# Tree attention on one core: twelve partitions of three stores go to SyncE's queue, and turn 17 has one transposition instead of two

## The chip, the cores and the metric

The kernel runs on one core of a Trainium2 chip. Its time is the device time of one execution in microseconds (us), and less is better. Three runs of the kernel before gave 132.96 us as their median (132.62 to 134.33).

## What is computed

Inputs are Q, K and V of shape (8, 12, 512, 64) in 4-byte floats: 96 independent heads of 512 rows. Row i stands for a node of a binary tree, and it may look at itself and at its ancestors only:

```python
    for i in range(seq):
        mask[i, i] = 1
        parent = i
        while parent > 0:
            parent = (parent - 1) // 2
            mask[i, parent] = 1

    scores = np.einsum('bhqd,bhkd->bhqk', Q, K) * scale
    scores = scores + (1 - mask) * (-1e9)

    weights = np.exp(scores - np.max(scores, axis=-1, keepdims=True))
    weights = weights / (np.sum(weights, axis=-1, keepdims=True) + 1e-10)

    return np.einsum('bhqk,bhkd->bhqd', weights, V).astype(np.float32)
```

## The kernel before

A partition p of the 128 holds the four rows 4p to 4p + 3 of a head, so that a head's row of output is 1 KB in a partition. The 96 heads go in 48 pairs (index i in the code), and four pairs form a group of eight heads (g = i // 4).

**Loads.** POOL (GpSimd) issues nearly all transfers, in the order that the string POOL (L612) writes out. Each load of K, Q or V for eight heads (`load_coarse` at L262, `load` at L251) turns the 4-byte values into 2-byte ones on the way. POOL also copies in SBUF: parts of V are spread into the layout that the products need (`spread`, L306, tile vt), and K and Q of a group are laid side by side (`lay_beside`, L324, tiles Kbeside and Qbeside).

**Transpositions.** For a group, four steps T of eight transposes each on TensorE (PE) fill the PSUM tile kqp: two steps for the keys (L375) and two for the queries (L397). VectorE (DVE) copies the result to the SBUF tile kq: after each key step by a copy of 1024 elements a partition (L444), and after the second query step by one of 2048 (L436). There is no copy after the first query step. There is one buffer for kqp.

**Scores, values, norm.** A step S computes the scores of a pair in PSUM (L494, L499, L519, L525) and ScalarE (ACT) takes their exponentials (L510, L541). A step V multiplies them with V into the PSUM tile ob (L552), and DVE divides by the sums (L585, L590) into the SBUF tile `of`, one for each of the groups 0 to 10, and into a small tile `ol` for each of the last four pairs. There is one buffer for ob.

**The order.** The string EARLY (L726) writes out the first steps. From then on a loop over turns i (L767) does "S T V": scores of pair i, the next transposition in line, values of pair i - 1. TURNS (L727) replaces the order of single turns. With one T a turn, the transposition made in turn i is number i + 4, so that a group's last one falls in the turn just before the scores that read it. In the kernel before, turn 17 has two of them, "S T V T", and from turn 18 on the transposition of turn i is number i + 5; turn 43 has none left.

**Stores.** `store` (L597) writes the output of a group of eight heads, 1 MB, in one DMA. POOL issues the eleven of them, s0 to s10 in the string POOL, s0 behind the load v88 and the last ones when nothing else is left. The last four pairs are stored by `store_pair` (L604): two from POOL, one and a half from SyncE (SP), half a one from ACT. SP otherwise issues two small loads at the start.

Of the kernel before, what the change touches and what calls it, by code (L numbers as in the profile page):

```python
# [11 lines left out]
CODE_ROWS = 40  # L12
CODE_BITS = 16
NOUT = 10
COARSE = range(1, 12)
COARSE_K = range(1, 12)
BESIDE = {"K": range(3, 12), "Q": range(3, 12)}
# [104 lines left out]
def kernel(  # L122
# [7 lines left out]
    nc = tc.nc  # L130
    B, H, S, D = Q.shape
    P = nc.NUM_PARTITIONS
# [5 lines left out]
    KB, VB = 8, 16  # L138
# [13 lines left out]
    Or = out.rearrange("b h (p t) d -> p (b h) (t d)", t=4)  # L152
# [14 lines left out]
    small = ctx.enter_context(tc.tile_pool(name="small", bufs=4))  # L167
    opool = ctx.enter_context(tc.tile_pool(name="opool", bufs=NOUT))
    olast = ctx.enter_context(tc.tile_pool(name="olast", bufs=GP))
# [61 lines left out]
    def head(i, a):  # L231

        g, x = divmod(i, GP)
        return KB * g + GP * a + x if g in COARSE else 2 * i + a

# [13 lines left out]
    qTs, kTs, kqps, obs, ets, ofs = {}, {}, {}, {}, {}, {}  # L249
# [12 lines left out]
    def load_coarse(kept, name, src, h0, n):  # L262

        assert n == KB
        issued.update((name, h) for h in range(h0, h0 + n))
        to = kept[h0 // KB] = loads.tile([P, 2, 16, D], bf16, name=name)
        return nc.gpsimd.dma_start(
            out=to[:, :, :, :].rearrange("p g s d -> p g (s d)"),
            in_=src[32 * h0:32 * (h0 + n), :].rearrange("(g r) c -> r g c", g=2),
        )  # L270
# [6 lines left out]
    def load_q(h0, n):  # L277
        if h0 // KB in COARSE:
            return load_coarse(qsts, "qst", Qc, h0, n)
        return load(qsts, loads, "qst", KB, Qr, h0, n)  # L280
# [29 lines left out]
    def lay_beside(copy, name, g):  # L310
# [4 lines left out]
        src = kept[:, :, :, :].bitcast(mybir.dt.uint32)  # L315
        if g not in COARSE:
            src = src.rearrange("p (x a) t w -> p x t a w", a=2)
        elif name == "Q" or g in COARSE_K:
            src = src.rearrange("p a s w -> p s a w")
        else:  # L320
            src = src.rearrange("p (a x) t w -> p (x t) a w", a=2)
        if g in COARSE:
            dst = dst.rearrange("p x t a w -> p (x t) a w")
# [53 lines left out]
    def transpose_coarse(i):  # L377

        g, x = divmod(i, GP)
        kqps[i] = kqps[i - 1] if x == 3 else psT.tile([P, 2, 32, 32], bf16, name="kqp")  # L380
        if x < 2 and g in COARSE_K:
            assert all(("kst", h) in issued for h in range(KB * g, KB * g + KB))
            return transpose_rows(i, x)
        if x < 2:
            for half in range(2):
                transpose_keys(GP * g + 2 * x + half, kqps[i], half)
            return
        assert all(("qst", h) in issued for h in range(KB * g, KB * g + KB))
        for half in range(2):
            for y, t in enumerate(ORDER):  # L390
                four = 2 * x - 4 + half
                for rows, src in turned(
                    "Q", g, t, lambda b: b[:, four, t, :, :], lambda a: qsts[g][:, a, 4 * four + t, :]
                ):
                    u = 16 * half + y
                    dst = kqps[i][rows, x - 2, u:u + 13:4, :]
                    nc.tensor.transpose(out=dst, in_=src, identity=eye[:, 0:128])  # L397

    def transpose(i, halves=(0, 1)):
        g = i // GP  # L400
        if g in COARSE:
            return transpose_coarse(i)
# [18 lines left out]
    def evac(i):  # L421
# [5 lines left out]
        if g in COARSE_K:  # L427
            dst = kqgs[g][:, 1, 2 * (x % 2):2 * (x % 2) + 2, :, :]
        elif g in COARSE:
            dst = kqgs[g][:, 2 * (x % 2):2 * (x % 2) + 2, x // 2, :, :]  # L430
# [164 lines left out]
            )  # L595

    def store(eng, g):  # L597
        return eng.dma_start(  # L598
            out=Or[:, KB * g:KB * g + KB, :],
            in_=ofs[g][:, :, :, :].rearrange("p h t d -> p h (t d)"),  # L600
        )


    def store_pair(eng, i, a=0, n=2):  # L604
# [14 lines left out]
    def pool_program():  # L619

        ops = []
        for word in POOL.split():
            kind, *n = word[0], *(int(x) for x in word[1:].split(".") if x)
            if kind in "kqv":
                h0, size = n if len(n) == 2 else (n[0], KB)
                ops.append(({"k": load_k, "q": load_q, "v": load_v}[kind], h0, size))
            elif kind in "KQ":
                ops.append((lay_early if kind == "K" else lay_q, n[0]))
            elif kind == "c":
                o, part, h0, h1 = n  # L630
                ops.append((spread, nc.gpsimd.tensor_copy, o, part, h0, h1))
            elif kind == "t":
                o, h0 = n
                ops += [
                    (spread, nc.gpsimd.tensor_copy, o, part, h0, h0 + KB)
                    for part in (6, 7, 8, 9) + ((), (4, 5))[min(o, 1)]
                ]
            elif kind == "s":
                ops.append((store, nc.gpsimd, n[0]))
            elif kind == "p":  # L640
                ops.append((store_pair, nc.gpsimd, n[0]))
            elif kind == "e":
                ops.append((eye_order,))
            else:
                ops.append((code_order, n[0]))
        return ops
# [77 lines left out]
        kept[0] = loads.tile([P, KB, 4, D], bf16, name=name)  # L724
        nc.vector.tensor_copy(out=kept[0][:, 0:2, :, :], in_=first[src][:, :, :, :])
    EARLY = "X K S Q D0 S A0 X6 T X D1 S X T V S T V T V T T A4 S D3 T V S T V"  # L726
    TURNS = {11: 'S T L4 V', 17: 'S T V T'}  # L727
    done, scored, valued = 1, 0, 0
    pool(-1)
    transpose(0)  # L730
# [36 lines left out]
    for i in range(scored, NP + 1):  # L767
        turn = "S T V" if i not in TURNS else TURNS[i]
        for token in turn.split():
# [39 lines left out]
```

## Time and profile before

| What | Value |
|---|---|
| Median of three runs | 132.96 us (132.62 to 134.33) |
| The profiled execution, its time | 132.84 us |
| The profiled execution, its span from first to last instruction | 130.8 us |
| Mean granted TensorE clock | 0.986 |
| PE busy | 115.4 us, 88% of the span |
| ACT busy | 99.0 us, 76% |
| POOL busy | 96.3 us, 74% |
| DVE busy | 95.9 us, 73% |
| DMA packets of POOL's queue | 30.67 MB moved, 23232 packets |
| Share of the chain that ended last | PE 59%, DVE 25%, POOL 6% |

The profile shows one execution. PE is the matmul unit, PEld its weight loads; SPq, POOLq and ACTq are the queues from which an engine issues. A row of a timeline has the start, the length, the engine, the line of the program, what is written and read, and a count; a bracket at its end names the idle time of the engine ahead of it and what ended that. In a table of stretches, a row has the stretch, its length, the busy time of PE, PEld, DVE, ACT and POOL with their counts of instructions, the granted clock of PE, the mean busy share of the 16 DMA engines (transfers overlap in an engine, so that it can be over 1) and the GB/s that they moved.

### The profile page before, as it was taken

What the parts mean: (1) busy time and instruction counts of PE and PEld (TensorE: products, weight loads), DVE (VectorE), ACT (ScalarE), POOL (GpSimd) and SP (SyncE); (2) the same over time, 40 slices, a digit from 0 to 9 for tenths busy, and PEclk for the clock granted to TensorE, in tenths of its full rate; (3) what the DMA queues carried; (4) which work ended last, traced back from release to release, by engine and by line L of the source; (5) the groups of instructions that cost most, each with busy time, mean ns of one, the idle gap of its engine ahead of it and who ended that gap; (6) DMA issues with size and microseconds to landing.
All of it is one profiled execution on the core that took longest, in us unless ns stands there. A gap on an engine that the chain in (4) does not pass through costs nothing.

```text
span 130.8 us, 4949 instructions
## 1 busy us (share of the span) xinstructions
PE 115.4 (88%) x2132; PEld 82.6 (63%) x2133; DVE 95.9 (73%) x179; ACT 99.0 (76%) x160; POOL 96.3 (74%) x149
## 2 busy tenths in 40 slices
PE   4989996999998998995999997989989999989930
PEld 1444565776866676774776875767767777856620
DVE  4236778758958959774989798798998898775460
ACT  4339553787988988886778886887897897899920
POOL 6979978239899999999999999999996930202300
PEclk9999999999999999999999999999999999999995
DMA  4999999999999999999999999999999999999992
GB/s 124 195 185 205 209 185 211 201 211 205 210 197 217 201 206 202 209 205 207 212 199 211 202 209 207 205 210 232 336 220 357 406 401 401 401 402 401 384 352 94
DMA packets 24533, 32.13 MB, mean 246 GB/s; under 512 B 944, under 2 KB 15920, under 8 KB 24512
## 3 DMA queue, kind: packets, MB, share of 16 engines
q0 software_dynamic: 23232, 30.67, 110.9%
q1 hardware_dynamic: 720, 0.70, 1.7%
q10 hardware_dynamic: 560, 0.46, 1.0%
q8 instruction: 16, 0.26, 0.7%
q14 instruction: 5, 0.04, 0.1%
HBM read 37.86 MB, written 12.58 MB: 385 GB/s over the span
## 4 chain that ended last, share of the span: by engine, by line
PE 59%; DVE 25%; POOL 6%; issue 3%; ACT 3%; ACTq 0%; POOLq 0%
PE ob L552 16%; DVE kq L436 7%; PE s L494 7%; DVE of L590 7%; PE kqp L375 7%; PE s L499 6%; PE kqp L397 6%; PE s L519 5%; DVE vt L306 5%; PE s L525 5%; PE s L718 3%; POOL vt L306 3%; PE ob L718 2%; PE kqp L350 2%; DVE rec L585 2%
## 5 line engine op out<-in xcount | busy, mean ns | idle before, releaser
L510 ACT ACTIVATE e<-s 128x1024 bf16<-128x1024 f32 x48 | 49.1, 1023 | 21.3 <-PE s L499 20.9
L306 POOL COPY vt<-vst 32x256 uint32<-32x256 uint32 (+2 forms) x70 | 34.9, 499 | 8.9 <-DMA vst<-in_V_dram 5.7
L541 ACT ACTIVATE e<-s 128x384 bf16<-128x384 f32 (+1 forms) x92 | 41.4, 505 | 0.0
L552 PE MATMUL ob<-vt,e 128*128 128x65 bf16 (+1 forms) x940 | 36.9, 197 | 2.4 <-DVE of L590 2.1
L552 PEld LDWEIGHTS <-e 128*128 128x128 bf16 (+1 forms) x960 | 31.2, 102 | 7.9 <-DVE of L590 3.7
L590 DVE TENSOR_TENSOR of<-ob,rec 128x512 f32<-128x512 f32 x44 | 30.4, 691 | 1.5
L306 DVE COPY vt<-vst 32x512 uint32<-32x512 uint32 (+1 forms) x33 | 20.6, 625 | 1.0
L499 PE MATMUL s<-kq 64*128 64x512 bf16 x96 | 18.4, 379 | 2.1 <-DVE kq L436 2.1
L525 PEld LDWEIGHTS <-kq 64*128 64x128 bf16 x384 | 16.3, 110 | 6.3
L598 POOL DMA_DIRECT2D out_dram<-of x11 | 9.8, 897 | 13.5 <-DVE of L590 13.5
L585 DVE RECIPROCAL rec<-ob 128x8 f32<-128x8 f32 x47 | 9.6, 204 | 12.8 <-PE ob L552 12.5
L444 DVE COPY kq<-kqp 128x1024 bf16<-128x1024 bf16 x22 | 15.1, 687 | 4.9 <-PE kqp L375 4.4
L525 PE MATMUL s<-kq 64*128 64x160 bf16 (+1 forms) x384 | 17.9, 210 | 0.0
L494 PE MATMUL s<-qcoarse,codes 40*128 40x512 bf16 x88 | 17.2, 387 | 0.0
L519 PE MATMUL s<-qcoarse,codes 40*128 40x480 bf16 x88 | 16.3, 364 | 0.3
L436 DVE COPY kq<-kqp 128x2048 bf16<-128x2048 bf16 x11 | 13.5, 1224 | 2.2 <-PE kqp L397 1.8
L375 PE MATMUL kqp<-mixed,Kbeside 128*128 128x128 bf16 x144 | 11.1, 220 | 2.8 <-POOL Kbeside L324 1.7
L519 PEld LDWEIGHTS <-codes 40*128 40x128 bf16 x96 | 7.6, 95 | 8.4 <-issue 2.0
L306 ACT COPY vt<-vst 32x512 uint32<-32x512 uint32 (+1 forms) x17 | 10.7, 627 | 1.7 <-DMA vst<-in_V_dram 1.3
L397 PE MATMUL kqp<-ptile,Qbeside 128*128 128x128 bf16 x144 | 11.2, 220 | 0.2 <-DVE kq L444 0.2
L375 PEld LDWEIGHTS <-Kbeside 128*128 128x128 bf16 x144 | 8.3, 98 | 4.2 <-POOL Kbeside L324 2.0
L257 POOL DMA_DIRECT2D vst<-in_V_dram x12 | 10.9, 910 | 0.0
(45 smaller groups left out, 102.2 us busy)
## 6 DMA issues: line engine op xcount, KB each, us to landing
out_dram<-of POOLq DMA_DIRECT2D x11, 1024.0 KB, 15.6
vst<-in_V_dram POOLq DMA_DIRECT2D x12, 512.0 KB, 14.0
kst<-in_K_dram POOLq DMA_DIRECT2D x11, 512.0 KB, 11.9
qst<-in_Q_dram POOLq DMA_DIRECT2D x11, 512.0 KB, 12.3
out_dram<-ol POOLq DMA_DIRECT2D x2, 256.0 KB, 5.3
qst<-in_Q_dram POOLq DMA_DIRECT2D x3, 128.0 KB, 7.1
ol<-in_K_dram SPq DMA_DIRECT2D x1, 256.0 KB, 2.9
ol<-in_Q_dram ACTq DMA_DIRECT2D x1, 256.0 KB, 3.2
```

Source lines behind the costliest of these rows:

```text
L306: return copy(out=dst, in_=src)
L375: nc.tensor.transpose(out=dst, in_=src, identity=perm)
L397: nc.tensor.transpose(out=dst, in_=src, identity=eye[:, 0:128])
L436: return nc.vector.tensor_copy(out=dst, in_=src) if x == 3 else None
L494: nc.tensor.matmul(out=columns(g, sp[:, a, :], 0, 512), lhsT=k1code[64 * a:64 * a + CODE_ROWS, :], rhs=query_codes(i, a, 0, 0, 512), start ...
L499: nc.tensor.matmul(out=columns(g, sp[:, a, :], 0, 512), lhsT=keys(i, a, TOP), rhs=queries(i, a, 0, 512), start=False, stop=True,)
L510: nc.scalar.activation(out=dst, in_=src, func=AF.Exp, scale=scale)
L519: nc.tensor.matmul(out=columns(g, flat[:, a, :], 32, 512), lhsT=k2code[64 * a:64 * a + CODE_ROWS, :], rhs=query_codes(i, a, 1, 32, 512), s ...
L525: nc.tensor.matmul(out=columns(g, flat[:, a, :], lo, hi), lhsT=keys(i, a, TILE2[t]), rhs=queries(i, a, lo, hi), start=False, stop=t == 1,)
L541: nc.scalar.activation(out=dst, in_=src, func=AF.Exp, scale=scale)
L552: nc.tensor.matmul(out=ob[lo:hi, a, 65 * t:65 * t + 65], lhsT=e[:, a, PLACE[t], lo:hi], rhs=vt[:, head(i, a) % VB, tile_v, 0:D + 1], **flags,)
L590: nc.vector.tensor_tensor(out=dst, in0=o4[:, a:a + n, :, 0:D], in1=rec[:, a:a + n, :, :].to_broadcast([P, n, 4, D]), op=ALU.mult,)
```

## The change

`store` splits the store of the groups 1, 4 and 7 (`SPLIT`) in three. The engine that is given, POOL in all cases, issues the first 116 partitions. SyncE issues partitions 116 to 121 and 122 to 127, with a DMA for each six. The other eight group stores stay whole. The DMAs of SyncE wait for the data on SyncE's own queue.

The entry for turn 17 leaves TURNS, so that turn 17 is "S T V" as most are. The first query step of group 5 that stood there moves to turn 18, each later transposition moves one turn back, and turn 43 gets the last one.

```diff
+SPLIT = (1, 4, 7)
...
     def store(eng, g):
-        return eng.dma_start(
-            out=Or[:, KB * g:KB * g + KB, :],
-            in_=ofs[g][:, :, :, :].rearrange("p h t d -> p h (t d)"),
-        )
+        rows = ((eng, 0, 116), (nc.sync, 116, 122), (nc.sync, 122, 128)) if g in SPLIT else ((eng, 0, P),)
+        for eng, lo, hi in rows:
+            eng.dma_start(
+                out=Or[lo:hi, KB * g:KB * g + KB, :],
+                in_=ofs[g][lo:hi, :, :, :].rearrange("p h t d -> p h (t d)"),
+            )
...
-    TURNS = {11: 'S T L4 V', 17: 'S T V T'}
+    TURNS = {11: 'S T L4 V'}
```

## The prediction

> **What bounds the kernel now.** I read the table of stretches first: it has the busy time of each engine, the share of the DMA engines and their GB/s side by side.
>
> ```profile
> HBM read 37.86 MB, written 12.58 MB: 385 GB/s over the span
> ```
> ```profile
> 70.00:80.00 10.00, 9.22 (x181) 7.12 (x180) 8.68 (x16) 8.97 (x16) 9.68 (x14) 1.00 1.21 207
> 100.00:110.00 10.00, 9.96 (x199) 7.61 (x196) 8.59 (x17) 8.93 (x15) 4.61 (x6) 1.00 1.03 402
> 110.00:120.00 10.00, 9.28 (x181) 6.62 (x177) 7.37 (x15) 8.94 (x16) 0.89 (x1) 1.00 1.03 403
> ```
> ```profile
> 124.00:125.00 1.00, 1.00 (x30) 0.82 (x25) 0.34 (x2) 1.00 (x3) 0.62 (x1) 1.00 0.98 381
> 125.00:126.00 1.00, 0.61 (x14) 0.40 (x12) 0.88 (x3) 0.05 (x1) 0.00 (x0) 1.00 0.90 356
> 126.00:126.50 0.50, 0.00 (x0) 0.00 (x0) 0.47 (x3) 0.00 (x0) 0.00 (x0) 1.00 0.57 223
> 126.50:127.00 0.50, 0.00 (x0) 0.00 (x0) 0.34 (x1) 0.00 (x0) 0.00 (x0) 1.00 1.02 379
> 127.00:127.50 0.50, 0.00 (x0) 0.00 (x0) 0.00 (x0) 0.00 (x0) 0.00 (x0) 0.61 1.03 375
> 127.50:128.00 0.50, 0.00 (x0) 0.00 (x0) 0.00 (x0) 0.00 (x0) 0.00 (x0) 0.50 0.83 297
> 128.00:128.50 0.50, 0.00 (x0) 0.00 (x0) 0.00 (x0) 0.00 (x0) 0.00 (x0) 0.50 0.57 199
> 128.50:129.00 0.50, 0.00 (x0) 0.00 (x0) 0.00 (x0) 0.00 (x0) 0.00 (x0) 0.50 0.34 117
> 129.00:129.50 0.50, 0.00 (x0) 0.00 (x0) 0.00 (x0) 0.00 (x0) 0.00 (x0) 0.50 0.17 57
> 129.50:130.00 0.50, 0.00 (x0) 0.00 (x0) 0.00 (x0) 0.00 (x0) 0.00 (x0) 0.50 0.00 0
> ```
>
> The column before the last is the mean busy share of the 16 DMA engines, the last one their GB/s. Loads turn 4-byte values into 2-byte ones, so 207 GB/s moved are twice that read; stores move 402 to 403 GB/s. Both are about the same traffic, the share stays at about 1 until 125, and the 50.4 MB of inputs and outputs would need 50.4 / 0.403 = 125 us. Transfers bound this kernel from the first loads on. The last rows matter most: after 127.5 nothing computes, and the share falls 0.83, 0.57, 0.34, 0.17. The DMA engines do not end together. The work after 126.0 is 0.5 x (0.57 + 1.02 + 1.03 + 0.83 + 0.57 + 0.34 + 0.17) = 2.27 us an engine; shared out evenly it would end at 128.3, and the last engine ends at about 129.5. So an average engine has 1.2 us of room before the end moves, and 1.2 us is all that a better sharing could gain.
>
> Next the timeline of the end, to see when the compute side lets go, and the list of DMA issues with the time from issue to landing:
>
> ```profile
> 120.10 0.89 POOL L598 DMA_DIRECT2D out_dram<-of  x1 [7.49 <-DVE of L590]
> 122.07 0.71 POOL L607 DMA_DIRECT2D out_dram<-ol  x1 [1.08 <-DVE ol L590]
> 123.89 0.72 POOL L607 DMA_DIRECT2D out_dram<-ol  x1 [1.12 <-DVE ol L590]
> ```
> ```profile
> 126.41 0.42 DVE L590 TENSOR_TENSOR ol<-s,rec 128x256 f32<-128x256 f32 x1
> 126.87 0.35 ACTq L607 DMA_DIRECT2D out_dram<-ol  x1
> ```
> ```profile
> out_dram<-of POOLq DMA_DIRECT2D x11, 1024.0 KB, 15.6
> out_dram<-ol ACTq DMA_DIRECT2D x1, 128.0 KB, 3.1
> ptile<-tree_eye ACTq DMA_DIRECT2D x1, 64.0 KB, 2.2
> ```
>
> A store of eight heads lands 15.6 us after its issue though its 1 MB is 2.6 us of work at 403 GB/s: it stands in line. The last store (128 KB, issued at 126.87) lands at 126.87 + 3.1 = 130.0. A 64 KB transfer with nothing ahead of it took 2.2 us, so without a line the last one, 64 KB more at 403 GB/s, would take some 2.4 and land near 129.3: compute may be about 0.7 us later before it counts.
>
> **The change, part by part.** The sum is made against the profiled execution, 132.84 us, with a span of 130.8; the median of the three runs is 132.96, 0.12 above. About 2.9 us lie between the last landing and 132.84, and I leave them as they are.
>
> Bytes. Three stores keep 116 of 128 rows on POOL's queue; 12 rows x 8 heads x 1 KB = 96 KB each, 288 KB in all, go through SyncE. Nothing is added or dropped, so the mean work of a DMA engine stays. Only its sharing changes. A full store is 64 KB for each of 16 engines, 2.6 us at 403 / 16 = 25.2 GB/s.
>
> SyncE's six added DMAs: there is no row of a six-row DMA. One end: it is spread over all 16 engines, and the sharing stays as it is, 0 us. Other end: one row of 8 KB to an engine, so six engines. If these are the same six each time they get 3 x 2 x 8 KB = 48 KB, 48 x 1.024 / 25.2 = 2.0 us more. If the 116 rows left stay even over all 16, each engine has 288 / 16 = 18 KB less, 0.7 us: the six end at +1.3. If those rows go by eights, 14 engines keep 64 KB, one has half and one nothing: the six keep their +2.0, one engine loses 3.9 us and one 7.8. So a six-engine split gives +1.3 to +2.0 on the six, against 1.2 us of room on an average engine: the end moves by +0.1 to +0.8 when they are average ones, by 0 when they are early ones, by the full +1.3 to +2.0 when the very last is among them. I take +0.2, near the low end, because the rows after 127.5 show room for most engines (at 128.5 already two thirds are done), and keep -1.2 and +2.0 as bounds.
>
> The Trainium skill, page "DMA: Bandwidth & Descriptors", section "Why a DMA increments its semaphore by 16 and not by 1", says that a DMA from SyncE uses the largest number of engines up to 16 that divides its slowest dimension, the lowest-numbered ones. By it a six-row DMA runs on the first six engines, always the same, and the sum would take the +1.3 to +2.0 on them; no row here names an engine.
>
> When SyncE issues them. SP's own queue is empty between the first loads and the end:
>
> ```profile
> 1.55 0.34 SPq L191 DMA_DIRECT2D codes<-tree_codes  x1
> 125.59 1.08 SPq L607 DMA_DIRECT2D out_dram<-ol  x2
> ```
>
> so each pair of DMAs waits only for its last normalisation and does not wait for POOL's place in line. Heads 8 to 15 are complete with the row at 34.42, those of the fifth group near 65.8, those of the eighth near 93.1:
>
> ```profile
> 34.42 0.69 DVE L590 TENSOR_TENSOR of<-ob,rec 128x512 f32<-128x512 f32 x1
> 65.06 0.69 DVE L590 TENSOR_TENSOR of<-ob,rec 128x512 f32<-128x512 f32 x1
> 92.39 0.69 DVE L590 TENSOR_TENSOR of<-ob,rec 128x512 f32<-128x512 f32 x1
> ```
>
> Six issues at 0.35 us (as 126.87's) cost 2.1 us of an idle queue: nothing. Behind them waits only SP's last pair of stores at 125.59, 30 us later. The loads that run at 35 and 66 are delayed on the six engines by 16 KB, 0.65 us. POOL waits there and later only twice:
>
> ```profile
> 35.93 3.08 POOL L306 COPY vt<-vst 32x256 uint32<-32x256 uint32 x6 [0.51 <-DMA vst<-in_V_dram]
> 101.23 1.04 POOL L324 COPY Qbeside<-qst 128x1024 uint32<-128x1024 uint32 x1 [1.12 <-DMA qst<-in_Q_dram]
> ```
>
> The first can grow by 0.65 at most; the second feeds transposes that PE reaches at 111.4 (below), 9 us later. I cost both at nothing. POOL's store keeps its issue of some 0.9 us (rows above); with 12 rows fewer it can hardly shrink, and if it took 1.8 the three would cost 2.7 us of POOL, which stands idle for 7.49 us ahead of the last such store. Nothing.
>
> Turn 17. The diff removes one step (eight transposes and, for this index, no copy), which turn 43 gets back: PE's work stays. From turn 18 on each transposition comes one turn later. Rows of PE's timeline, with the wait in brackets:
>
> ```profile
> 41.53 0.41 PE L499 MATMUL s<-kq 64*128 64x512 bf16 x2 [0.38 <-DVE kq L436]
> 53.47 0.38 PE L499 MATMUL s<-kq 64*128 64x512 bf16 x2
> 55.59 0.61 PE L397 MATMUL kqp<-ptile,Qbeside 128*128 128x128 bf16 x8 [0.17 <-DVE kq L444]
> 60.77 0.62 PE L375 MATMUL kqp<-mixed,Kbeside 128*128 128x128 bf16 x8 [1.50 <-POOL Kbeside L324]
> 79.01 0.61 PE L375 MATMUL kqp<-mixed,Kbeside 128*128 128x128 bf16 x8 [0.54 <-DVE kq L436]
> 79.86 0.78 PE L552 MATMUL ob<-vt,e 128*128 128x65 bf16 x20 [0.24 <-DVE of L590]
> 82.91 0.38 PE L499 MATMUL s<-kq 64*128 64x512 bf16 x2
> 85.03 0.38 PE L499 MATMUL s<-kq 64*128 64x512 bf16 x2
> 111.34 0.62 PE L397 MATMUL kqp<-ptile,Qbeside 128*128 128x128 bf16 x8
> 117.17 0.38 PE L499 MATMUL s<-kq 64*128 64x512 bf16 x2
> ```
>
> A turn without a wait takes 85.03 - 82.91 = 2.12. From turn 17 (53.47) to turn 44 (117.17) are 27 turns: 63.70 - 27 x 2.12 = 6.5 us of waits and of the extra step. What goes: the 1.50 at 60.77, since that transposition then comes a turn (2.1 us) after the copy it needs, and the waits like 0.54 + 0.24 at 79. What comes: in seven groups (5 to 11) the copy L436 is now made in the turn just before the scores that need it, as before turn 17, where those scores wait 0.38 (longest of such waits 1.0, "PE s L499" below); with the rest of such a turn I price 0.6. 7 x 0.6 = 4.2 instead of 6.5: compute ends some 2 us earlier, or, at 1.0 each, 0.5 later.
>
> ```profile
> PE s L499 <- DVE kq L436: 2.1, 4, 1.0
> ```
>
> Behind that wait stand PE's next transposes and products and ACT's exponentials; late next are the last stores' issues. Either way it lies beside the transfers, whose engines are full until 125; an earlier end only fills the 0.43 of idle share in 126.0 to 126.5 on engines that are early anyhow. 0 us.
>
> Sum: 132.84 + 0.2 + 0 = 133.0 us.
>
> **The rivals.**
> (B) Late engines get the added rows. The share of 0.57 in 128.0 to 128.5 says that about nine of 16 are still busy then; six unlucky ones of 16 include a late one easily. The end moves by the whole +1.3 to +2.0, less some room: 133.6 to 134.8. Against it: only that an order of the engines may favour the six.
> (C) The relieved engines are the late ones and the six early ones: the end falls by 0.3 to 1.2, to 131.6 to 132.5. For it: by eights, the two engines that lose 3.9 and 7.8 us would leave the tail. The gain stops where the next late engine ends. The Trainium skill, page "DMA: Bandwidth & Descriptors", section "Latency and other measured facts", holds engines 7 and 15 to be usually slower; by that rule, and rows by eights, engine 15 would be the one with nothing. No run here shows which engine is which.
> (D) Slower than before: 116 does not split over 16 engines, and POOL's store runs on few. On four engines, 29 rows each are 232 KB, 9.4 us instead of 2.6. If the three stores take different fours, most engines have 9.4 in place of 3 x 2.6 = 7.8, and with SyncE's 2.0 the worst has 3.6 more: 136.4; if the same four, over 150. It decides once an engine gets more than 1.2 us over the average. Against: the bytes of a row are cut into 1 KB pieces, 928 of them, which 16 divides. The stores of before all have 128 rows and tell nothing on this. The Trainium skill, page "DMA: Bandwidth & Descriptors", section "Why a DMA increments its semaphore by 16 and not by 1", gives the rule of divisors, by which 116 rows go to four engines; it also tells of copies from POOL that keep 16 engines and go by eights. No run here shows either.
> (E) Compute becomes the bound: each of the seven waits costs 1.0 or more, or the added wait in turn 20 and POOL's later copies add up beyond the 0.7 us of room. At 1.5 each, 10.5 - 6.5 - 0.7 = 3.3 over: 136.1.
>
> **How the numbers follow.** Forecast (end moves by less than 0.7 either way, 132.3 to 133.6): 0.45. B 0.24, C 0.17, D 0.08, E 0.06. The range of 8 in 10 goes from 131.8 (most of C) to 134.8 (all of B), leaving out D and most of E. 2% of 132.96 is 2.66 us, about what a measurement of this kernel can tell from no change: faster needs under 130.3, below C's bound, 0.03; slower needs over 135.6, D and part of E, 0.10; the rest 0.87.
>
> **What would show it.** Right: DMA share near 1 until 125 again; SP rows at about 35, 66 and 93; the tail after 127.5 of about the same length; the wait of 1.50 at 60.77 gone and seven waits "PE s L499 <- DVE kq L436" more; the last DVE row earlier than 126.83. Wrong: a tail longer than 2 us with a low share (B, D), one that ends in a step with all engines (C), stores that land over 20 us after their issue (D), or a last DVE row after 127.5 with a DMA share well under 1 before it (E).

## The result and the profile after

| | before | after |
|---|---|---|
| Median | 132.99 us, six runs (132.62 to 134.33) | 149.59 us, six runs (148.99 to 151.07) |
| Profiled execution: time, span | 132.84, 130.8 | 149.17, 147.1 |
| Mean granted TensorE clock | 0.986 | 0.922 |

The ratio is 1.125, with an interval of 1.12 to 1.13: 16.6 us slower. The forecast was 133.0 with a range to 134.8; what happened is rival D, and at several times its price. Lines of the kernel after are one to three higher than before: `store` is L601, `store_pair` L610, the copies to kq L437 and L445.

First the page after, its lines on DMA: packets and bytes, packets by size, and the two queues with packets, MB and share of 16 engines. The same lines of before follow.

```profile
DMA packets 26873, 32.17 MB, mean 219 GB/s; under 512 B 3068, under 2 KB 18332, under 8 KB 26852
...
q0 software_dynamic: 25248, 30.41, 102.9%
q1 hardware_dynamic: 1044, 0.99, 2.2%
```
```profile
DMA packets 24533, 32.13 MB, mean 246 GB/s; under 512 B 944, under 2 KB 15920, under 8 KB 24512
...
q0 software_dynamic: 23232, 30.67, 110.9%
q1 hardware_dynamic: 720, 0.70, 1.7%
```

The bytes are nearly the same, but POOL's queue (q0) has 2016 packets more although it moves less. The records by size hold 2088 packets of 16 bytes where before had none: 3 x 12 x 58. And a store of 116 rows is 928 KB, 232 packets of 4 KB, which is 4 x 58. So each of the three stores gives 58 packets of data, 29 rows, to four engines, and 58 packets of 16 bytes to each of the other twelve. The trace also has sixteen events for the landing of each DMA from POOL. Read as one event for each engine, they agree: for the store s1 before they come from 100.6 to 104.1, and after twelve come from 99.8 to 104.9 and four from 110.4 to 116.7. SyncE's queue (q1) has 324 more: 288 of 1 KB, the 288 KB, and 36 small ones, one for each of six engines and six DMAs. The Trainium skill, page "DMA: Bandwidth & Descriptors", section "Why a DMA increments its semaphore by 16 and not by 1", has the rule of the largest divisor up to 16: 116 goes to four, 6 to six. The packets agree. Its exception, copies from POOL that keep all 16 engines, did not hold for this one.

The table of stretches after, from 100 on, with the last two columns as before (share of the 16 DMA engines, GB/s):

```profile
100.00:105.00 5.00, 5.00 (x101) 3.79 (x100) 4.68 (x10) 4.32 (x9) 4.90 (x5) 1.00 1.00 280
105.00:110.00 5.00, 4.64 (x90) 3.48 (x89) 4.37 (x6) 4.11 (x7) 4.22 (x4) 1.00 0.90 285
110.00:115.00 5.00, 4.81 (x97) 3.61 (x94) 4.11 (x10) 4.25 (x8) 0.00 (x0) 1.00 0.94 283
115.00:120.00 5.00, 3.57 (x65) 2.33 (x63) 3.50 (x6) 3.53 (x6) 1.79 (x2) 1.00 0.76 222
120.00:125.00 5.00, 4.24 (x46) 2.60 (x47) 0.90 (x2) 2.44 (x4) 1.33 (x2) 0.58 0.91 309
125.00:130.00 5.00, 4.57 (x76) 3.12 (x74) 2.15 (x6) 2.93 (x6) 0.97 (x2) 0.74 0.81 226
130.00:135.00 5.00, 0.00 (x0) 0.00 (x0) 0.77 (x3) 0.00 (x0) 0.00 (x0) 0.60 0.78 266
135.00:140.00 5.00, 0.00 (x0) 0.00 (x0) 0.00 (x0) 0.00 (x0) 0.00 (x0) 0.50 0.76 294
140.00:145.00 5.00, 0.00 (x0) 0.00 (x0) 0.00 (x0) 0.00 (x0) 0.00 (x0) 0.50 0.30 117
```

and of before the two rows that the prediction did not show:

```profile
120.00:125.00 5.00, 4.87 (x102) 3.45 (x98) 2.14 (x6) 4.80 (x9) 2.32 (x3) 1.00 0.99 387
125.00:130.00 5.00, 0.61 (x14) 0.40 (x12) 1.68 (x5) 0.05 (x1) 0.00 (x0) 0.71 0.63 236
```

The transfers end near 145 instead of 129.5, 15.5 us later, and the share column splits this in two. From 100 on an average engine is busy 20 x 1.03 + 5 x (0.99 + 0.63) = 28.7 us before, and 5 x (1.00 + 0.90 + 0.94 + 0.76 + 0.91 + 0.81 + 0.78 + 0.76 + 0.30) = 35.8 us after: 7.1 us more of being busy, for nearly the same bytes (11.2 MB before, 11.4 after, by GB/s x time). And it idles 29.5 - 28.7 = 0.8 us before, 45.0 - 35.8 = 9.2 us after (3.4 of them ahead of 130): 8.4 more. So there are two losses of like size: packets that take longer (283 GB/s at a share of 0.94, where 402 at 1.03 stood), and engines that have nothing to do while others are late. The records of POOL's 4 KB packets say what "longer" means. From 100 on their median is 165 ns in both kernels, but 16% of them take over 200 ns after, and 0.6% before. Some packets wait, then; no record says for what. Between 135 and 140 the share of 0.76 at 294 GB/s is three quarters of both: twelve engines at full rate, four with nothing left. Three stores with four engines each, and twelve late engines: the fours were different ones. The landing events agree: four of sixteen are late for s1, eight for s4 (eight until 112.0, the others from 118.7), twelve for s7 (four until 121.1, the others from 127.6).

One reason of the idle time before 130 stands in POOL's timeline. POOL's later stores before and after, with the idle time ahead in brackets:

```profile
102.22 3.52 POOL L598 DMA_DIRECT2D out_dram<-of  x4
111.73 0.89 POOL L598 DMA_DIRECT2D out_dram<-of  x1 [6.00 <-DVE of L590]
```
```profile
86.69 1.98 POOL L601 DMA_DIRECT2D out_dram<-of  x1
...
101.15 2.09 POOL L601 DMA_DIRECT2D out_dram<-of  x1
...
105.46 3.76 POOL L601 DMA_DIRECT2D out_dram<-of  x3
117.05 1.79 POOL L601 DMA_DIRECT2D out_dram<-of  x2 [7.83 <-DVE rec L586]
120.39 0.89 POOL L601 DMA_DIRECT2D out_dram<-of  x1 [1.54 <-DMA out_dram<-of]
```

Store s8, the last of the four at 102.22 before, goes out at 117.05 after. Its data had been there for over ten microseconds, so the engine in the bracket is not the reason. The list of issues for 84 to 93 names the candidate, s1, issued at 86.69 (columns as before):

```profile
out_dram<-of POOLq DMA_DIRECT2D x1, 928.0 KB, 30.0
```

86.69 + 30.0 = 116.7: s8 goes out when s1 has landed, s1 being late by its four engines. What holds it is a wait of the program. By the records, POOL's DMAs signal their landing on eight semaphores (counters that an instruction can wait for), numbers 99 to 106 in turn, and whichever takes a number over waits for the DMA that had it. The number of s1, 99, comes round to s9, eight DMAs later, and the wait for it stands ahead of s8 (count, duration in ns, start):

```profile
L601 POOLq EVENT_SEMAPHORE  x1: 17/17/17, 117.0 to 117.0; - x1
```

In the kernel before the same wait was over at 104.1, when s1 had landed. So one uneven store keeps back whole ones behind it, and engines that could work idle. The issue of a 116-row store takes 2.0 us instead of 0.9.

The compute side is not what ends late, though it too ends later:

```profile
120.76 0.61 PE L500 MATMUL s<-kq 64*128 64x512 bf16 x1 [1.80 <-issue]
```
```profile
130.38 0.42 DVE L591 TENSOR_TENSOR ol<-s,rec 128x256 f32<-128x256 f32 x1
```

PE stands 1.80 us, to which the trace gives no releaser, and its granted clock is 0.58 from 120 to 125 (table above). A late load of code would fit the stall: a 16 KB packet of the queue for instructions (q8) starts at 118.35, 11.7 us behind the one ahead of it, where they are 6 to 9 us apart in the later part of the kernel before, and PE goes on 1.5 us after its end. In e1 below, PE stands 2.63 us and goes on 1.3 us after the end of such a packet. That this is the cause is not shown. The last DVE row is 4.0 us later than before's 126.41, and the transfers run 15 us beyond it.

### The profile page after: what moved, and what is told of

It reads as the page before. It is cut to its first block, busy times and chain, and to the rows that moved or that the text cites. A ratio compares the mean times of both kernels' runs of the same rounds, so it can differ in the third digit from the quotient of the medians.

```text
span 147.1 us, 4962 instructions
## 1 busy us (share of the span) xinstructions
PE 117.4 (80%) x2133; PEld 84.1 (57%) x2133; DVE 96.4 (66%) x179; ACT 99.0 (67%) x160; POOL 100.1 (68%) x149
## 3 DMA queue, kind: packets, MB, share of 16 engines
HBM read 37.86 MB, written 12.58 MB: 343 GB/s over the span
## 4 chain that ended last, share of the span: by engine, by line
PE 52%; DVE 18%; DMA 12%; issue 3%; POOL 3%; ACT 1%; POOLq 0%
PE ob L553 14%; DVE kq L437 8%; PE s L500 7%; PE kqp L398 7%; PE s L495 6%; DMA qst<-in_Q_dram 6%; PE s L526 6%; DMA kst<-in_K_dram 6%; PE kqp L376 6%; PE s L520 5%; DVE vt L307 3%; DVE of L591 3%; DVE kq L445 1%; POOL kst L258 1%; POOL qcoarse L246 1%
## 5 line engine op out<-in xcount | busy, mean ns | idle before, releaser
L307 POOL COPY vt<-vst 32x256 uint32<-32x256 uint32 (+2 forms) x70 | 35.4, 505 | 11.1 <-DMA vst<-in_V_dram 8.0
L553 PE MATMUL ob<-vt,e 128*128 128x65 bf16 (+1 forms) x940 | 37.7, 199 | 1.2 <-DVE of L591 0.7
L553 PEld LDWEIGHTS <-e 128*128 128x128 bf16 (+1 forms) x960 | 32.1, 104 | 6.1 <-DVE of L591 1.4
L500 PE MATMUL s<-kq 64*128 64x512 bf16 x96 | 19.7, 393 | 7.1 <-DVE kq L437 5.3
L526 PEld LDWEIGHTS <-kq 64*128 64x128 bf16 x384 | 17.3, 112 | 7.1 <-issue 1.3
L601 POOL DMA_DIRECT2D out_dram<-of x11 | 13.2, 1203 | 9.4 <-DVE rec L586 7.8
L526 PE MATMUL s<-kq 64*128 64x160 bf16 (+1 forms) x384 | 19.0, 214 | 0.0
L520 PE MATMUL s<-qcoarse,codes 40*128 40x480 bf16 x88 | 17.6, 379 | 0.2 <-ACT e L542 0.2
L437 DVE COPY kq<-kqp 128x2048 bf16<-128x2048 bf16 x11 | 13.5, 1225 | 5.5 <-PE kqp L398 5.4
L445 DVE COPY kq<-kqp 128x1024 bf16<-128x1024 bf16 x22 | 15.1, 685 | 2.9 <-PE kqp L376 2.6
L500 PEld LDWEIGHTS <-kq 64*128 64x128 bf16 x96 | 6.7, 110 | 11.2 <-issue 10.6
L398 PE MATMUL kqp<-ptile,Qbeside 128*128 128x128 bf16 x144 | 11.2, 220 | 0.0
L376 PE MATMUL kqp<-mixed,Kbeside 128*128 128x128 bf16 x144 | 11.2, 220 | 0.0
## 6 DMA issues: line engine op xcount, KB each, us to landing
qst<-in_Q_dram POOLq DMA_DIRECT2D x3, 128.0 KB, 8.5
```

Of the source, the lines that this page charges most:

```text
L307: return copy(out=dst, in_=src)
L376: nc.tensor.transpose(out=dst, in_=src, identity=perm)
L437: return nc.vector.tensor_copy(out=dst, in_=src) if x == 3 else None
L500: nc.tensor.matmul(out=columns(g, sp[:, a, :], 0, 512), lhsT=keys(i, a, TOP), rhs=queries(i, a, 0, 512), start=False, stop=True,)
L520: nc.tensor.matmul(out=columns(g, flat[:, a, :], 32, 512), lhsT=k2code[64 * a:64 * a + CODE_ROWS, :], rhs=query_codes(i, a, 1, 32, 512), s ...
L526: nc.tensor.matmul(out=columns(g, flat[:, a, :], lo, hi), lhsT=keys(i, a, TILE2[t]), rhs=queries(i, a, lo, hi), start=False, stop=t == 1,)
```

## The experiments

Theories at the start: **four engines** (POOL's 116-row stores run on four engines each), **SyncE** (its six-row DMAs load six engines, or disturb POOL's), **turn 17** (the waits for kq). A fourth came up on the way: **cut rows** (any cut of a store's rows makes packets slow). Diffs are against the kernel after. Three of the runs (e5, e11, e16) scatter too widely for an interval, so they have a median and their extremes only.

**e1: the split alone.**

```diff
-    TURNS = {11: 'S T L4 V'}
+    TURNS = {11: 'S T L4 V', 17: 'S T V T'}
```

> The split of the three stores as in the changed kernel, with the second transposition of turn 17 put back. Theory 1 (POOL's 116-row stores run on four of the 16 DMA engines) and theory 2 (SyncE's six-row DMAs overload a few engines): the whole loss stays, 148.5 to 151 us. Theory 3 (the transpositions one turn later): the loss goes, 132.5 to 133.5.

Measured: 151.27 us against 132.62, ratio 1.138 (1.132 to 1.145). Just above the forecast of theories 1 and 2.

**e2: turn 17 alone.**

```diff
-SPLIT = (1, 4, 7)
+SPLIT = ()
```

> All stores whole, turn 17 with one transposition. Theories 1 and 2: 132.3 to 133.5 us, as the transfers bound the kernel; the wait of 1.50 us at 60.77 goes and the last VectorE row comes 0 to 2 us earlier than 126.83. Theory 3: 148 to 150.

Measured: 132.86 us against 132.62, ratio 1.003 (0.999 to 1.007). The whole loss is the split's. The trace of e2 has the effect of turn 17 undisturbed: the waits of PE for the copy L437 (total, times, longest; before 2.1, 4, 1.0), in e2 and in the kernel after, and the last DVE row of e2.

```profile
PE s L500 <- DVE kq L437: 4.9, 10, 1.1
```
```profile
PE s L500 <- DVE kq L437: 5.3, 11, 1.1
```
```profile
125.28 0.42 DVE L591 TENSOR_TENSOR ol<-s,rec 128x256 f32<-128x256 f32 x1
```

Compute ends 1.1 us earlier than before and the time does not move.

**e3: 112 rows on POOL, twice eight on SyncE.** 112 splits evenly over 16 engines.

```diff
-        rows = ((eng, 0, 116), (nc.sync, 116, 122), (nc.sync, 122, 128)) if g in SPLIT else ((eng, 0, P),)
+        rows = ((eng, 0, 112), (nc.sync, 112, 120), (nc.sync, 120, 128)) if g in SPLIT else ((eng, 0, P),)
```

> The changed kernel with the cut at row 112: POOL 112 rows, SyncE two DMAs of eight rows. 112 divides by 16. Theory 1: no added time from POOL's stores, 132.5 to 135 us (SyncE's eight engines get 48 KB more each, POOL's engines 24 KB less: about +1), POOL's issue near 0.9 us and no 16-byte packets. Theory 2: SyncE moves a third more, so the loss stays or grows, 148 us or more.

Measured: 139.97 us, ratio 1.054 (1.048 to 1.059). The 16-byte packets are gone, and so is over half of the loss, but not all. So the divisor is not all: theory 1 gave 135 at most, and what is left is another loss. Its stretch:

```profile
110.00:120.00 10.00, 9.26 (x179) 6.81 (x177) 6.49 (x13) 8.34 (x15) 1.77 (x2) 1.00 1.01 354
```

The engines are all busy (1.01) and move 354 GB/s where before moved 403: slower packets with no idle time. From 100 on, 7% of POOL's 4 KB packets take over 200 ns.

**e4: one store cut, not three.**

```diff
-SPLIT = (1, 4, 7)
+SPLIT = (4,)
```

> The changed kernel with one split store, group 4, in place of three. Theory 1: four engines have 232 KB of this store and nobody evens it out, so the end moves by 232 - 64 = 168 KB at 25.2 GB/s = 6.8 us at least, up to 10 with slower packets: 139 to 143.5 us, that is, over a third of the loss for a third of the stores. Theory 2, or a loss that adds up by stores: a third of 16.6, 138.5.

Measured: 148.95 us, ratio 1.120 (1.111 to 1.129): one store costs as much as three, and both theories gave less (143.5 at most). Its end shows why:

```profile
105.00:110.00 5.00, 4.62 (x92) 3.56 (x90) 4.31 (x8) 3.96 (x7) 1.17 (x3) 1.00 1.04 255
...
130.00:132.00 2.00, 0.00 (x0) 0.00 (x0) 0.00 (x0) 0.00 (x0) 0.72 (x1) 0.50 0.50 195
132.00:134.00 2.00, 0.00 (x0) 0.00 (x0) 0.00 (x0) 0.00 (x0) 0.00 (x0) 0.50 0.27 104
134.00:136.00 2.00, 0.00 (x0) 0.00 (x0) 0.00 (x0) 0.00 (x0) 0.00 (x0) 0.50 0.26 101
136.00:138.00 2.00, 0.00 (x0) 0.00 (x0) 0.00 (x0) 0.00 (x0) 0.00 (x0) 0.50 0.15 59
...
144.00:146.00 2.00, 0.00 (x0) 0.00 (x0) 0.00 (x0) 0.00 (x0) 0.00 (x0) 0.50 0.06 25
```

From 132 a share of a quarter at a quarter of the rate: four engines, then two, then one. Each of the four carries 232 KB instead of 64, 168 x 1.024 / 25.2 = 6.8 us more. They end between 136 and 147, so more than this is lost on them. The landing events of the split store say on how many: twelve come until 111.5, the others at 118.1, 119.2, 125.7 and 129.5. Two engines are late by about the 6.8 us, two by some 14 and 18; for these two no run shows the reason. The wait for a semaphore keeps back only POOL's very last store here, until 130.02, so that the loss is almost wholly that of the four late engines. At the moment when the store goes through, 105 to 110, the share is 1.04 at 255 GB/s: slow packets again (5% of the 4 KB packets from 100 on). On which engines they fall, the records do not tell.

**e5: all three parts on POOL's queue.**

```diff
-        rows = ((eng, 0, 116), (nc.sync, 116, 122), (nc.sync, 122, 128)) if g in SPLIT else ((eng, 0, P),)
+        rows = ((eng, 0, 116), (eng, 116, 122), (eng, 122, 128)) if g in SPLIT else ((eng, 0, P),)
```

> The changed kernel with the six-row DMAs issued by POOL too, so that SyncE has no part in it. Theory 1 (POOL's 116-row DMA uses four engines): the loss stays, 146 to 153 us. Theory 2 (the loss is SyncE's six-row DMAs on the same few engines): it goes for the most part, 133 to 137.

Measured: 167.23 us (164.03 to 168.25), before 133.44. Without SyncE it is worse, so its queue is not the cause, though the six-row DMAs are still there, issued by POOL. Theory 1 gave 153 at most; it lacked that each added DMA also takes one of POOL's eight semaphores, so that the number of a late store comes round sooner:

```profile
115.97 4.41 POOL L601 DMA_DIRECT2D out_dram<-of  x4 [7.89 <-DMA out_dram<-of]
123.22 0.57 POOL L601 DMA_DIRECT2D out_dram<-of  x1 [2.85 <-DMA out_dram<-of]
136.53 2.71 POOL L601 DMA_DIRECT2D out_dram<-of  x3 [12.74 <-DMA out_dram<-of]
```

Here the brackets name it: POOL waits for the landing of stores before it issues the next, 23.5 us in these three. Each goes out within 0.6 us of the landing of the DMA whose semaphore it takes over.

**e6: 120 rows on POOL** (four and four on SyncE: `(eng, 0, 120), (nc.sync, 120, 124), (nc.sync, 124, 128)`).

> The cut at row 120: POOL 120 rows, SyncE two DMAs of four rows. By a rule of divisors (the largest number up to 16 that divides the rows) POOL's store runs on 15 engines with eight rows each: 133 to 135.5 us. If whatever does not divide by 16 falls back to four engines or fewer: about 149. If, as the 112-row run suggests, other rows to an engine than those of a whole store slow the packets by themselves (theory 1b): 137 to 143.

Measured: 142.9 us, ratio 1.067 (1.054 to 1.080). 120 is 15 x 8, and the records show small packets for one idle engine a store only (48 in three stores). So the divisor gives the engines rightly, but the 133 to 135.5 us worked out from it fell, and theory 1b (137 to 143) held: 11% of the 4 KB packets take over 200 ns.

**e9: 112 and 16 rows, both on POOL** (`(eng, 0, 112), (eng, 112, 128)`).

> The cut at row 112 with both parts on POOL's queue, 112 and 16 rows, both of which divide by 16. If the 7 us of the 112-row run came from SyncE's eight-row DMAs (theory 2): 132.5 to 134 us. If they come from POOL's 112 rows, seven to an engine, which lie across the rows that other engines read in whole stores (theory 1b): 137 to 142, with q0's busy share times span grown by 1 engine-us or more against its 145.1.

Measured: 140.35 us, ratio 1.038 (1.024 to 1.051), 334 GB/s at a share of 1.00 from 110 to 120. A like loss without SyncE.

**e10: cut by heads.** POOL stores seven heads of all 128 rows, SyncE the eighth.

```diff
-        rows = ((eng, 0, 116), (nc.sync, 116, 122), (nc.sync, 122, 128)) if g in SPLIT else ((eng, 0, P),)
-        for eng, lo, hi in rows:
+        parts = ((eng, 0, 7), (nc.sync, 7, 8)) if g in SPLIT else ((eng, 0, KB),)
+        for eng, lo, hi in parts:
             eng.dma_start(
-                out=Or[lo:hi, KB * g:KB * g + KB, :],
-                in_=ofs[g][lo:hi, :, :, :].rearrange("p h t d -> p h (t d)"),
+                out=Or[:, KB * g + lo:KB * g + hi, :],
+                in_=ofs[g][:, lo:hi, :, :].rearrange("p h t d -> p h (t d)"),
             )
```

> The same three stores shared by heads in place of rows: POOL seven heads of all 128 rows, SyncE the eighth head of all 128 rows (128 KB, more than the 96 KB of the change). All 16 engines get the same. Theories 1 and 1b: 132.3 to 133.5 us. If a share for SyncE costs by itself (theory 2 in its wide form): 137 or more.

Measured: 133.61 us, ratio 0.999 (0.994 to 1.004).

```profile
110.00:120.00 10.00, 9.46 (x182) 6.70 (x178) 6.95 (x14) 8.87 (x17) 1.42 (x2) 1.00 1.03 404
```

128 KB a store leave POOL for SyncE, more than in the change, and it costs nothing: neither a second queue nor a cut store is dear by itself.

**e11: halves, 0 to 64 and 64 to 128, both on POOL** (`(eng, 0, 64), (eng, 64, 128)`).

> The three stores cut in halves of 64 rows, both on POOL's queue, four rows to an engine. If a cut of the rows slows the packets whenever the DMA has other than all 128 rows: 137 to 143 us, GB/s from 110 to 120 well under 400 at a DMA share of 1. If only blocks of rows that are no power of two (seven, eight of 120) do it: 132.5 to 134, near 400 GB/s.

Measured: 141.97 us (138.56 to 145.42), before 133.67.

```profile
110.00:120.00 10.00, 9.61 (x190) 7.08 (x186) 7.00 (x14) 8.85 (x15) 1.51 (x2) 1.00 1.00 342
```

Both halves use all engines (no packets of 16 bytes), and still 10% of the 4 KB packets take over 200 ns.

**e13: all eleven stores cut**, 112 rows on POOL and 16 on SyncE (`SPLIT = tuple(range(11))`, `(eng, 0, 112), (nc.sync, 112, 128)`).

> All eleven stores of eight heads cut at row 112, 112 rows from POOL and one DMA of 16 rows from SyncE. If the slow packets come from engines that read the same rows at once because cut and whole stores share the rows out differently (mixing): with nearly all stores cut alike they are fewer, 133 to 139 us. If a cut store is slow by itself: 7 us for three give some 25 for eleven, 150 to 160.

Measured: 140.79 us, ratio 1.051 (1.040 to 1.062), 322 GB/s at 1.00: no dearer than three cut stores, though its packets are no faster (13% take over 200 ns). Both forecasts missed: mixing was to make slow packets fewer, and a price by the store was to give 150 or more.

**e14: one store cut so** (`SPLIT = (4,)`, the same rows).

> Only the store of group 4 cut at row 112, with 16 rows from SyncE. A cost that adds up by cut stores: a third of 7, 134.5 to 136 us. Mixing theory: the lag that one cut store gives an engine stays and whole stores behind it run no slower, 134 to 137. No cost at all: 133.

Measured: 135.22 us, ratio 1.012 (1.007 to 1.017).

```profile
110.00:120.00 10.00, 9.45 (x184) 7.00 (x185) 6.82 (x15) 9.08 (x16) 1.77 (x2) 1.00 1.02 393
```

Both forecasts hold, so this run does not choose between them. Beside e4 it is the price of the four engines: the same store, cut at 112 instead of 116, loses 1.6 us instead of 16. (SyncE's part differs too: 16 rows in one DMA, not twelve in two; the twelve give six engines 16 KB each, 0.65 us.)

**e16: all eleven stores in halves** (`SPLIT = tuple(range(11))`, halves as e11), and **e17: three stores in even and odd rows**, both parts on POOL. Still open then was why cuts that use 15 or 16 engines cost anything.

```diff
-        rows = ((eng, 0, 116), (nc.sync, 116, 122), (nc.sync, 122, 128)) if g in SPLIT else ((eng, 0, P),)
-        for eng, lo, hi in rows:
+        rows = ((eng, 0, 2), (eng, 1, 2)) if g in SPLIT else ((eng, 0, 1),)
+        for eng, lo, by in rows:
             eng.dma_start(
-                out=Or[lo:hi, KB * g:KB * g + KB, :],
-                in_=ofs[g][lo:hi, :, :, :].rearrange("p h t d -> p h (t d)"),
+                out=Or[lo:P:by, KB * g:KB * g + KB, :],
+                in_=ofs[g][lo:P:by, :, :, :].rearrange("p h t d -> p h (t d)"),
             )
```

> All eleven stores are cut into rows 0 to 64 and 64 to 128, both halves on POOL; turn 17 as in the changed kernel. Theory of the mixture (packets slow only because cut and whole stores share the DMA engines with different orders of rows): all are cut alike, so the rate from 110 to 120 is near 400 GB/s again and the time 132 to 136 us. Theory that any store of fewer than 128 rows slows its own packets and its neighbours': rate 345 GB/s or below, 140 to 147 us, no better than the 142 us of three cut stores. Theory of the ports (a half of the partitions reaches only half of the ports to SBUF): as the second, 142 us or more, since every store then runs at half of the ports.

> Stores 1, 4 and 7 are each cut into even and odd partitions, 64 rows each, both on POOL; turn 17 as in the changed kernel. Theory of the ports: each of the two DMAs reaches all of the partitions' ports, so most of the loss of the cut into upper and lower halves (142 us) is gone: 133 to 137 us, and 380 GB/s or more from 110 to 120. Theory that any store of fewer than 128 rows slows the packets, whichever rows they are: 140 to 145 us and 330 to 350 GB/s, as for the two halves. Theory of the mixture: the same 140 to 145 us.

Measured: e16 136.59 us (133.89 to 136.99); e17 133.23 us, ratio 1.002 (0.998 to 1.005); before 132.82. Their rows, e16 first:

```profile
110.00:120.00 10.00, 9.46 (x192) 7.03 (x190) 6.91 (x14) 9.08 (x16) 3.48 (x6) 1.00 1.02 367
```
```profile
110.00:120.00 10.00, 9.46 (x180) 7.18 (x179) 8.14 (x17) 8.20 (x15) 0.89 (x1) 1.00 1.02 400
```

e11 and e17 have the same stores, queue, number of DMAs and bytes in each; only which rows go together differs, and the cost goes from some 8 us to nothing. So neither the cut, nor a DMA of 64 rows, nor the added DMA makes packets slow: the choice of consecutive rows does. The packets agree: 0.8% of the 4 KB packets take over 200 ns in e17, 0.5% in e10, 8% in e16. Why it does is not settled. The ports' forecast held for e17 and missed for e16 (142 or more). The mixture's missed twice: for e16 narrowly in time (136 at most) and clearly in rate (367, not near 400), and for e17 (140 to 145). A third reading is that an engine that takes the same rows in every store does not meet other engines at them, and that even and odd rows or a cut by heads leave that so, while consecutive rows do not. It fits e10 and e17, but not by itself e13 and e16, where all eleven stores are cut alike and packets are slow. The Trainium skill, page "DMA: Bandwidth & Descriptors", section "The descriptor swizzle", gives each engine eight rows of its own behind one port in a transfer to 128 partitions; the stores here go the other way. The records name neither engine nor row, so this reading is argued, not shown. A fourth one is untested: consecutive rows are neighbours in DRAM as well as in SBUF, and no run changes only one of the two.

## Why the prediction was wrong, point by point

- **What bounds the kernel: right.** Transfers do, at a share near 1 until 125, with little room for uneven work: e2 ended compute 1.1 us earlier for nothing. (One reading beside it is the wrong way round: 37.86 MB read and 12.58 written make 32.1 MB moved, so that what the loads read is twice the 207 GB/s that they move.) That "an average engine has 1.2 us of room" fits too: in e4 four engines that are late by 7 to 18 us move the end by 16.
- **"If the 116 rows left stay even over all 16 … If those rows go by eights": the step that failed.** The part on the change took the 116 rows left as even, or by eights, and priced only SyncE's six engines. They went to four engines. That case stood among the rivals as D with a chance of 0.08, because "the bytes of a row are cut into 1 KB pieces, 928 of them, which 16 divides"; the split goes by rows, not by bytes. The rule of the Trainium skill that spoke against the change was quoted there and given too little weight, and no row of before could speak for either.
- **D's price was too low, 136.4 against 149.6.** "On four engines, 29 rows each are 232 KB, 9.4 us instead of 2.6" and "different fours" are what the packets, the landing events and the share of 0.76 show. But D added up bytes only. What it lacked: slower packets (most of the 7.1 us more that an average engine is busy), and the wait of POOL, which kept s8 back until s1 had landed 30 us after its issue (at most the 3.4 us of idle time ahead of 130). What each of them adds to the end, no run separates. That bytes do not tell the whole can be seen on the four engines that end early: by D's sum they have 7.8 us less to do than before, and yet they report s10 from 128.0 to 130.6, where before all sixteen did so from 124.5 to 127.3.
- **SyncE's six DMAs, "+0.2": the wrong item.** Six engines each, as bounded, at 35.62, 65.1 and 92.6 as forecast (35, 66, 93). By e5 SyncE's queue is not the loss, the landing events count four late engines a store and not six, and e10 moves more through SyncE for nothing.
- **POOL's issue: priced at nothing, and it "can hardly shrink".** It grew, from 0.9 to 2.0 us. The issue itself did not matter; what POOL waits for ahead of it did.
- **Turn 17: right in mechanism and in effect.** The wait of 1.50 on Kbeside is gone and seven more waits for L437 are there (11 after, 4 before), 5.3 us in all, 3.2 more; priced at 0.6 each with the rest of such a turn, measured 0.46 each. Compute ended 1.1 us earlier in e2, where 2 was forecast, and the time did not move. In the changed kernel this cannot be seen: there compute ends 4.0 us later.
- **Signs to look for.** A tail with a low share and stores that land over 20 us after their issue had been named for D, and both are there (0.76 to 0.30, and 30.0 us).
- **Chances.** 0.10 for slower was too little: four of five cases were sums over the bytes alone.

## What to carry to other kernels

Before rows of a store are given to another queue, factor the number of rows that stay: in this kernel 116 ran on four of the 16 engines and one such store cost 16 us, 112 on all 16 and one cost 1.6. Where a queue is full to the end, cut a transfer along another dimension (heads, e10) or in every second row (e17), both free here, rather than in consecutive rows, and look up which later DMAs wait for the landing of an uneven one: here they share eight semaphores, so that one late store held up the DMAs some eight places behind it. None of the versions tried beats the kernel before; with transfers at 402 GB/s and a share of 1, moving stores between queues had little to win.

## What the runs showed of the hardware that was not expected

- In a store from POOL that uses four engines, the other twelve get as many packets as the four have, of 16 bytes each (2088 in three stores), and its issue takes 2.0 us instead of 0.9.
- A late DMA stops its issuer by way of the program's semaphores, with no sign that the queue itself is full: a wait for the number that s1 and s9 share ends at 104.1 before and at 117.0 after, and in e5 three such waits take 23.5 us.
- DMA engines can be fully busy at 322 to 367 GB/s instead of 402 (e3, e9, e11, e13, e16), by nothing but which rows a DMA has. The median 4 KB packet takes 165 ns all the same (164 in e13); the slow ones, over 200 ns, grow from 0.6% to between 7 and 13%. The cost is not the sum over stores: one cut of 112 rows 1.6 us, three 7.4, eleven 7.1.
- PE's granted clock was 0.58 from 120 to 125 in the kernel after, behind a stall of 1.80 us whose reason is not shown.
